# A hybrid decoder layer on one core: the conv tiles' sum on other queues, half-wide products in pairs, the square root's table at other places

## The chip, the cores and the metric

The kernel runs on one core of one Trainium2 chip. A core has a matrix engine (TensorE, "PE" in the profile; its weight loads are the row "PEld"), a vector engine (VectorE, "DVE"), an activation engine (ScalarE, "ACT"), GpSimd ("POOL") and SyncE ("SP"), which here only issues DMAs. Each engine takes its instructions strictly in the order in which the program gives them, and engines wait for each other through semaphores. DMAs are issued from SP, ACT or POOL and run on 16 DMA engines. The metric is the device time of one execution in microseconds (us).

## The reference

One layer with batch 1, 1024 tokens and width 1024, all in float32:

```
h = rmsnorm(x) * (1 + scale(c)) + shift(c)
cv, cg, cs, lx, ls = split(h @ W_in)            # five times 1024 columns
v = layernorm(causal_conv31(cv * sigmoid(cg)))  # depthwise, 31 taps
y_conv = (silu(v) @ pw2 + b) * silu(cs)
xs = causal_conv4(lx)
r, i = sigmoid(blockdiag(xs)), sigmoid(blockdiag(xs))
a = exp(-8 r softplus(-lam))
y_lru = scan(a, sqrt(1 - a^2) * i * xs) * silu(ls)
x = rmsnorm(x + (1 + gate(c)) * (concat(y_conv, y_lru) @ W_out))
```

## The kernel before

**Layout.** Channels lie on the 128 partitions and the 1024 tokens along them, so that a matrix of 1024 channels is eight tiles of 128 x 1024. Tiles come from pools: 47 `big` buffers, two buffers each for a slot's weights (`raw`, `whi`, `wlo`), three PSUM tiles `mm` of two banks and two PSUM tiles `acc` of one bank.

**Products.** To keep float32's precision each operand is split into a rounded part and a remainder (`uh`, `ul`; `whi`, `wlo`), and a product is three matmuls: hi x hi, hi x lo, lo x hi. A *slot* is one tile of 128 output columns: 8 k-tiles x 3 terms x 2 halves = 48 matmuls of 512 columns (L506). For a slot's weights SP loads `raw`, ACT casts it to `whi` (L355), and the remainder `wlo` is a subtraction on POOL (slots under `EARLY` = 20), on DVE (under `LATE` = 41), or, in the last slots, ACT writes -`whi` into `wlo` and POOL issues a DMA that adds the source from DRAM (`remainder`, L387).

**Stages.** First four tiles of W_in are multiplied while x arrives, with the norm's factor applied later. The factor is found on the way: squares, a matmul with ones (`token_stats`), a square root on ACT (`root`), a reciprocal on DVE, a matmul that spreads it (L934), a copy to `rbc`; a fifth accumulation (`late`) follows. Then come slots 4 to 39 in the sequence `ORDER` ("i24" is column tile 24 of W_in, "g0" the gates of head 0), slots 40 to 47 (the lru half of W_out, from `yh`, `yl`), and then pw2 and the conv half of W_out as pairs of tiles, with seven half-size products for eight (tiles `xpw`, `zpw`, `ypw`, `xout` and so on). Column tiles 0-7 are conv values, 8-15 their gates, 16-23 `cs`, 24-31 `lx`, 32-39 `ls`.

**Conv.** Each of eight conv tiles is taken apart into even and odd tokens. Five accumulate their taps on DVE (`cacc`, `caccs`). Tiles 1, 3 and 5 (`POOLED`, function `conv_pooled`) do it by DMA: ACT writes each tap's product into a buffer (`cq`, both halves; `co`, one half of a buffer), and POOL issues a DMA that adds it to `es` or `oo` (function `ADD`, L387). `conv_sum` then adds the eight tiles into `csum`, in the order 2, 3, 0, 1, 7, 4, 5, 6: POOL does all additions but the last, DVE that one. `layer_norm` splits `csum`, finds the mean with a matmul, subtracts it, sums the squares in `lnss`, and takes a square root (`rstd`) for the factor `lnbc`.

**The order.** All this is first written down as operations with a priority, a cost and their reads and writes. At build time the class `Plan` plays them through in modelled time: whenever an engine is free it takes, of the operations that are ready and find free buffers, the one with the lowest priority number, and that becomes the program's order on each engine. So a changed cost or dependency can move any operation of any engine. `LAND` is the flight that the plan takes for a remainder's DMA, `FLIGHT` that of the other adding DMAs, `SWITCH` that of a table load on ACT; `reserve` asks for free `big` buffers beyond the operation's own; conv operations have priorities from 1000 up, slots their number. Activation functions come in table sets, and where a function needs another set than the one loaded, an ACT_TABLE_LOAD stands before it.

Lines: L355 copies and casts on ACT, L363 activations and their table loads, L374 scalar_tensor_tensor on DVE, L382 tensor_tensor on DVE or POOL, L387 adding DMAs on POOL, L401 DMAs on SP, L506 slots, L675 pair products, L799 first products, L981 the product `psbias` that sums `fsum`, L1205 gate products, L1242 the layer norm's mean.

Of the kernel before, what the change touches and what calls it, by code (L numbers as in the profile page):

```python
# [77 lines left out]
SUMS = (2, 3, 0, 1, 7, 4, 5, 6)  # L78
QRES = 0
# [13 lines left out]
LATE, LAND = 41, 4.5  # L93
# [32 lines left out]
class Plan:  # L126
# [4 lines left out]
    SWITCH = 1.3  # L131
# [56 lines left out]
    def order(self):  # L188
# [48 lines left out]
        while left:  # L237
# [3 lines left out]
            for e in engines:  # L241
# [29 lines left out]
                if o.table and o.table != table:  # L271
                    cost, table = cost + self.SWITCH, o.table
# [38 lines left out]
def hymba_layer(ctx: ExitStack, tc: tile.TileContext, xT, vecs, mod_w, w_first, w_in,  # L311
# [182 lines left out]
    def weights(s, after=(), n=None, eng=None, where=None, late=()):  # L494
        n = number[s] if n is None else n
        eng = eng or ("POOL" if n < EARLY else "DVE" if n < LATE else "DMA")
        w_bufs(s, where)
        w_slice(s, 0, KT, n - 2.5, n - 1.4, after, eng, late)
# [206 lines left out]
    def rstd(prio, sqs, a, e, ps, o, after=(), warm=(), idle=None):  # L705
# [20 lines left out]
        for k, sq in enumerate(sqs):  # L726
            at = S.op("PE", 0.18 * nb, lambda sq=sq, k=k: stats(sq, k), prio, halves(sq, a, e), wk,
                      after=after if k == 0 else [])
            for _ in range(warm[k] if warm else 0):
                S.op("PE", 0.22, warm_mm, prio, [], [idle], after=[at], columns=4 * P)  # L730
# [22 lines left out]
    ACT(-101, lambda: junk, lambda: eps_t, AF.Sqrt, 1, r=[("cs", 0)], w=[("junk", 0)])  # L753
# [229 lines left out]
    S.op("PE", 0.18 * len(FIRST + NEXT), shift_mm, BIP, [fsum], [psx])  # L983
# [25 lines left out]
    def softplus8(pr, after):  # L1009
        lam = lambda: V[:, OFF["lam"]:OFF["lam"] + KT]  # L1010
        u, s, s2, q, r = (S.buf("sp_" + n, "sp_" + n) for n in ("u", "s", "s2", "q", "r"))
        ACT(pr, u, lam, AF.Abs, KT, w=[u])
        ACT(pr, u, u, AF.Exp, KT, scale=-1.0, r=[u], w=[u])
# [91 lines left out]
    def conv_pooled(i, pr, ci, vi, src, wts, every):  # L1105
# [3 lines left out]
        es, oo, adds = big_buf(f"es{i}", parts=2), big_buf(f"oo{i}"), []  # L1109

        def product(to, z, r, x, key, scale, bias=None):
            ACT(pr, part(to, z * H + (0 if z else r), z * H + H), x,
                AF.Copy if bias is None else AF.Identity, H - (0 if z else r), bias=bias,
                scale=scale, r=[key, ("V", 1), ("wsum", 0)], w=[(to, z if to.parts > 1 else 0)],
                after=adds[-AHEAD:][:len(adds) // AHEAD][:1])
        for r in range(16):
# [3 lines left out]
            product(q, 1, r, part(ci, PAD - r, PAD - r + H), (ci, 0), ws(r),  # L1120
# [5 lines left out]
            q = oo if r == 0 else big_buf(f"co{i}_{r}")  # L1126
            product(q, 0, r, lambda r=r: od()[:, :H - r], vi, w(2 * r + 1))
            if r:
                adds.append(ADD(pr, part(oo, r, H), part(q, r, H), H, r=[oo, q], w=[oo]))
# [3 lines left out]
        def last(eng, o, a, e, src, off, op):  # L1133
            TT(pr, eng, lambda: every(o)()[:, a:e], lambda: every(o)()[:, a:e],
               part(src, off, off + e - a), op, e - a, r=[ci, src], w=[ci])
# [5 lines left out]
    def conv_sum():  # L1141
        for i in SUMS[1:]:
            a, eng = (c[SUMS[0]] if i == SUMS[1] else csum), "DVE" if i == SUMS[-1] else "POOL"
            TT(1000 + 5 * i, eng, csum, a, c[i], ALU.add, r=[a, c[i]], w=[csum])


    sig, sls, lru, y, scs_d, gw = {}, {}, {}, {}, {}, {}
    yh, yl = [None] * KT, [None] * KT
# [9 lines left out]
    def split(pr, hi, lo, full, eng="DVE", reserve=0):  # L1158
        ACT(pr, hi, full, "copy", r=[full], w=[hi], reserve=reserve and reserve + 1)
        SUB(pr, eng, lo, full, hi, r=[full, hi], w=[lo], reserve=reserve)  # L1160

    def evac_in(m, ps, n, b=None, rb=()):
# [15 lines left out]
        elif kind == LS:  # L1178
            sls[i] = big_buf(f"sls{i}")
            ACT(pr, sls[i], ps, AF.Silu, bias=b, r=[ps, *rb], w=[sls[i]])  # L1180
# [14 lines left out]
    def gates(i, n):  # L1195
# [27 lines left out]
        split(B0 - 2 + 0.2 * i, yh[i], yl[i], t, reserve=SPARE)  # L1223
# [11 lines left out]
    def layer_norm():  # L1235
# [9 lines left out]
        for t in range(KT):  # L1245
            TT(pr, "DVE", c[t], c[t], mean, ALU.subtract, r=[c[t], mean], w=[c[t]])
            if t == 0:
                ACT(pr, ss, c[t], AF.Square, r=[c[t]], w=[ss])
# [40 lines left out]
    n, started, acc_d = 3, {}, {}  # L1289
    for s in slots[4:]:  # L1290
# [5 lines left out]
        if s not in NEXT:  # L1296
            weights(s)
# [9 lines left out]
        for k in range(KT):  # L1307
            o = mm_k(n, ps, s, xh, xl, k, FULL)
            if k == 0:
                started[n] = o  # L1310
        if s[0] == "in":
# [6 lines left out]
            else:  # L1318
                evac_in(m, ps, n)
# [205 lines left out]
```

## Time and profile before

| | |
|---|---|
| median of 3 runs | 733.21 us (733.05 to 734.43) |
| profiled execution, its own time | 734.38 us |
| its span, first to last instruction | 732.5 us |
| granted TensorE clock, mean | 0.996 |
| busy: PE, PEld, DVE, ACT, POOL | 722.9, 601.2, 611.2, 459.4, 159.6 us |
| 16 DMA engines: moved over the span | 121.03 MB, mean 165 GB/s |
| ACT_TABLE_LOAD | 45, 1283 ns each |

The profile is of one execution. Its page gives busy times by engine, the span in 40 slices, the DMA queues, the chain of work that ended last, the costliest groups of instructions (line, engine, operation, out<-in names without buffer numbers) and the DMA issues. Rows of the timeline have the start, the length, the engine, the line, the operation, the tiles, their shape, the count of merged instructions, and in brackets the idle time before it with what ended it. A matmul's length includes its way through the pipeline, so successive matmuls overlap. The profiled execution's 734.38 us is 1.17 us above the median of the three runs.

### The profile page before, as it was taken

How to read it: one execution, taken by the hardware profiler on the slowest of the kernel's cores; microseconds unless marked ns; L12 is line 12 of the kernel's file. 1: busy time of each engine (PE TensorE's matmuls, PEld its weight loads, DVE VectorE, ACT ScalarE, POOL GpSimd, SP SyncE). 2: the span in 40 equal slices, each digit the busy share in tenths (PEclk: the TensorE clock that was granted, in tenths of full speed). 3: DMA queues.
4: the chain of work that ended last, by engine and by line, in shares of the span. 5: the costliest groups of instructions: out<-in, count | busy, mean ns of one | idle time of the engine just before them, and what ended most of it. 6: DMA issues, size and time to landing. Idle time of an engine off the chain costs nothing.

```text
span 732.5 us, 8976 instructions
## 1 busy us (share of the span) xinstructions
PE 722.9 (99%) x3292; PEld 601.2 (82%) x3292; DVE 611.2 (83%) x832; ACT 459.4 (63%) x579; POOL 159.6 (22%) x147
## 2 busy tenths in 40 slices
PE   9999999999999999999999999999999999999996
PEld 8888888888888887888888888888888888878885
DVE  7999999989559996888598999839698566999647
ACT  7650677656669759956848789517594345755322
POOL 0024012344524222232215111320000001010003
PEclk9999999999999999999999999999999999999998
DMA  8961023358888999799753644686666846784006
GB/s 342 408 223 58 0 82 84 86 115 191 196 209 183 239 243 215 179 224 211 161 114 85 154 90 120 173 233 174 170 158 152 227 117 138 221 217 167 20 15 216
DMA packets 40508, 121.03 MB, mean 165 GB/s; under 512 B 4496, under 2 KB 13200, under 8 KB 40464
## 3 DMA queue, kind: packets, MB, share of 16 engines
q0 software_dynamic: 15552, 43.70, 33.0%
q1 hardware_dynamic: 23904, 75.84, 30.3%
q10 hardware_dynamic: 1008, 0.92, 0.4%
q8 instruction: 26, 0.43, 0.2%
q14 instruction: 18, 0.15, 0.1%
HBM read 72.55 MB, written 12.58 MB: 116 GB/s over the span
## 4 chain that ended last, share of the span: by engine, by line
PE 69%; DVE 13%; issue 11%; DMA 3%; ACT 3%; POOL 1%; DVEq 0%; POOLq 0%; ACTq 0%
PE ps L506 46%; PE xout L675 5%; PE xpw L675 5%; PE ypw L675 3%; DVE modw L374 2%; DVE caccs L374 2%; PE gate L1205 2%; PE y L650 2%; PE zpw L675 1%; DMA wloout<-in_w_out_dram 1%; DVE ul L374 1%; DVE cacc L374 1%; PE zout L675 1%; DMA oo<-co 1%; DMA wlo<-in_w_out_dram 1%
## 5 line engine op out<-in xcount | busy, mean ns | idle before, releaser
L506 PE MATMUL ps<-uh,whi 128*128 128x512 f32 x576 | 177.6, 390 | 0.3 <-ACT scs L363 0.3
L506 PE MATMUL ps<-ul,whi 128*128 128x512 f32 x576 | 177.4, 389 | 0.0
L506 PE MATMUL ps<-uh,wlo 128*128 128x512 f32 x576 | 177.3, 389 | 0.0
L506 PEld LDWEIGHTS ps<-uh,whi 128*128 128x128 f32 x576 | 107.9, 188 | 23.3 <-ACT scs L363 1.0
L506 PEld LDWEIGHTS ps<-ul,whi 128*128 128x128 f32 x576 | 108.1, 188 | 22.5
L506 PEld LDWEIGHTS ps<-uh,wlo 128*128 128x128 f32 x576 | 108.1, 188 | 22.5
L355 ACT CAST whi<-raw 128x1024 fp32r<-128x1024 f32 x44 | 45.9, 1047 | 69.9 <-PE ps L506 44.9
L387 POOL DMA_DIRECT2D es<-cq x45 | 41.1, 936 | 128.0 <-ACT cq L363 91.7
L382 POOL TENSOR_TENSOR wlo<-raw,whi 128x1024 fp32r<-128x1024 f32 x16 | 40.3, 2530 | 126.0 <-ACT whi L355 85.1
L363 ACT ACT_TABLE_LOAD x45 | 57.7, 1283 | 5.8 <-DMA oo<-co 4.3
L374 DVE SCALAR_TENSOR_TENSOR cacc<-v,V,cacc 128x511 f32<-128x511 f32 (+14 forms) x75 | 55.6, 742 | 0.5
L374 DVE SCALAR_TENSOR_TENSOR caccs<-v,V,caccs 128x511 f32<-128x511 f32 (+6 forms) x70 | 52.1, 744 | 2.3 <-ACT caccs L363 1.1
L374 DVE SCALAR_TENSOR_TENSOR caccs<-c,wsum,caccs 128x511 f32<-128x511 f32 (+6 forms) x70 | 52.0, 743 | 1.0
L387 POOL DMA_DIRECT2D oo<-co x42 | 37.9, 948 | 61.7 <-ACT co L363 25.3
L506 PE MATMUL ps<-yh,wlo 128*128 128x512 f32 x128 | 39.6, 391 | 0.2 <-DMA wlo<-in_w_out_dram 0.2
L506 PE MATMUL ps<-yh,whi 128*128 128x512 f32 x128 | 39.6, 391 | 0.0
L506 PE MATMUL ps<-yl,whi 128*128 128x512 f32 x128 | 39.5, 389 | 0.0
L382 DVE TENSOR_TENSOR wlo<-raw,whi 128x1024 fp32r<-128x1024 f32 x21 | 27.5, 1311 | 5.8 <-ACT whi L355 5.8
L363 ACT ACTIVATE cq<-v,V 128x511 f32<-128x511 f32 (+14 forms) x45 | 31.8, 706 | 0.1
L374 DVE SCALAR_TENSOR_TENSOR xs<-ps,V,xs 128x1023 f32<-128x1023 f32 (+2 forms) x24 | 30.6, 1273 | 0.0
L374 DVE SCALAR_TENSOR_TENSOR modw<-modw,sc 128x1024 f32<-128x1024 f32 x23 | 30.1, 1312 | 0.0
L363 ACT ACTIVATE cq<-c,wsum 128x512 f32<-128x512 f32 x42 | 29.6, 711 | 0.0
(334 smaller groups left out, 1458.1 us busy)
## 6 DMA issues: line engine op xcount, KB each, us to landing
raw<-in_w_in_dram SPq DMA_DIRECT2D x36, 512.0 KB, 4.5
modw<-in_mod_w_dram SPq DMA_DIRECT2D x24, 512.0 KB, 7.9
scsd<-scs SPq DMA_DIRECT2D x8, 512.0 KB, 4.3
raw<-in_w_out_dram SPq DMA_DIRECT2D x8, 512.0 KB, 4.1
accd<-acc SPq DMA_DIRECT2D x8, 512.0 KB, 4.5
rawpw<-in_pw_dram SPq DMA_DIRECT2D x8, 512.0 KB, 4.1
scsr<-scsd SPq DMA_DIRECT2D x8, 512.0 KB, 4.9
rawout<-in_w_out_dram SPq DMA_DIRECT2D x8, 512.0 KB, 3.3
```

The costliest lines, as they stand in the source:

```text
L355: act.copy(out(), in_())
L363: act.activation(out=out(), in_=in_(), func=func, **kw)
L374: dve.scalar_tensor_tensor(out=out(), in0=in0(), scalar=scalar, in1=in1(), op0=op0, op1=op1, accum_out=accum)
L382: lambda: e.tensor_tensor(out=out(), in0=a(), in1=b(), op=op), prio, r, w,
L387: return S.op("POOL", ISSUE, lambda: pool.dma_start(out(), a(), accum_op=ALU.add), prio, r, w, lag=RATE * n / T, after=after, flight=flight)
L506: pe.matmul(ps()[:, a - off:b - off], k3(lhs)()[:, k, :], rhs[k]()[:, a:b], start=(k == 0 and lhs is wh and rhs is xh and (a - off) % H == 0),
L650: pe.matmul(to(), half(*lhs)()[:, j * P:j * P + P], half(*rhs)()[:, c0:c1], start=a == "S1" and j == 0 and t == 0, stop=j == KT // 2 - 1 a ...
L675: pe.matmul(half(ps, 0)(), half(*lhs)()[:, j * P:j * P + P], half(*rhs)(), start=start and j == 0 and t == 0, stop=j == KT // 2 - 1 and t ...
L1205: pe.matmul(ps()[:, c0:c1], lhs()[:, j, :], rhs()[:, c0:c1], start=st == 0, stop=st == 2)
```

## The change

- `conv_sum`: ACT copies conv tile 2 into `csum`; tiles 3, 0 and 1 are added by DMAs issued on POOL; tiles 7, 4, 5 and 6 (`CSD` = 4) are added on DVE. No tensor_tensor of POOL is left in the sum.
- `conv_pooled`: two odd-token products share one `big` buffer, one in each half (taps 0 and 1 in `oo` itself); ACT products ask for two spare `big` buffers (`CQR`).
- Softplus' Abs and Exp, which had the priority 35, get the priorities -129 and -128, and a one-element Sqrt (it loads the table) comes behind them, at -127. In `layer_norm` such a one-element Sqrt follows the first Square.
- The split of the lru outputs of heads 0 and 1 (`YHEADS`) waits for the start of slot 36 (`YSLOT`).
- Where an `ls` slot from slot 4 on is followed by gates, the ACT cast of the weights two and three slots on waits for that slot's evacuation (`pending_evac`).
- The plan's own figures: `LAND` 4.5 to 6.0, `SWITCH` 1.3 to 1.283 less the time that ACT has been idle, a one-column statistics matmul 0.18 to 0.224 us. The program's order is planned anew with all of this.

No matmul is added or removed, and `ORDER` is as it was. `EARLYD` is empty, so the kinds of remainders stay with their slots.

```diff
...
 SUMS = (2, 3, 0, 1, 7, 4, 5, 6)
+CSD = 4
+EVN = 4
+CQR = 2
+YHEADS, YSLOT = 2, 36
 QRES = 0
...
 EARLY = 20
-LATE, LAND = 41, 4.5
+EARLYD = ()
+LATE, LAND = 41, 6.0
 ISSUE, FLIGHT, RATE = 1.0, 10.0, 3.0
...
     LATENCY = {"SP": 2.0, "PE": 0.2, "ACT": 0.15, "DVE": 0.15, "POOL": 0.15}
-    SWITCH = 1.3
+    SWITCH = 1.283
     TICK, BUSY, COLD = 3.4133, 3060, 3.8
...
                 if o.table and o.table != table:
-                    cost, table = cost + self.SWITCH, o.table
+                    cost, table = cost + max(0.0, self.SWITCH - max(0.0, t - until[e])), o.table
                 if e == "PE":
...
         n = number[s] if n is None else n
-        eng = eng or ("POOL" if n < EARLY else "DVE" if n < LATE else "DMA")
+        eng = eng or ("DMA" if n in EARLYD or n >= LATE else "POOL" if n < EARLY else "DVE")
         w_bufs(s, where)
...
         for k, sq in enumerate(sqs):
-            at = S.op("PE", 0.18 * nb, lambda sq=sq, k=k: stats(sq, k), prio, halves(sq, a, e), wk,
+            at = S.op("PE", 0.224 * nb, lambda sq=sq, k=k: stats(sq, k), prio, halves(sq, a, e), wk,
                       after=after if k == 0 else [])
...
     ACT(-130, lambda: cs, lambda: V[:, OFF["c"]:OFF["c"] + KT], AF.Silu, KT, w=[("cs", 0)])
-    ACT(-101, lambda: junk, lambda: eps_t, AF.Sqrt, 1, r=[("cs", 0)], w=[("junk", 0)])
+    sp_u = S.buf("sp_u", "sp_u")
+    ACT(-129, sp_u, lambda: V[:, OFF["lam"]:OFF["lam"] + KT], AF.Abs, KT, w=[sp_u])
+    ACT(-128, sp_u, sp_u, AF.Exp, KT, scale=-1.0, r=[sp_u, ("cs", 0)], w=[sp_u])
+    ACT(-127, lambda: junk, lambda: eps_t, AF.Sqrt, 1, r=[sp_u], w=[("junk", 0)])
...
                       start=True, stop=True)
-    S.op("PE", 0.18 * len(FIRST + NEXT), shift_mm, BIP, [fsum], [psx])
+    S.op("PE", 0.224 * len(FIRST + NEXT), shift_mm, BIP, [fsum], [psx])
     ACT(BIP, lambda: bias, lambda: psx()[:, :len(FIRST + NEXT)], "copy", len(FIRST + NEXT), r=[psx],
...
         lam = lambda: V[:, OFF["lam"]:OFF["lam"] + KT]
-        u, s, s2, q, r = (S.buf("sp_" + n, "sp_" + n) for n in ("u", "s", "s2", "q", "r"))
-        ACT(pr, u, lam, AF.Abs, KT, w=[u])
-        ACT(pr, u, u, AF.Exp, KT, scale=-1.0, r=[u], w=[u])
+        u = sp_u
+        s, s2, q, r = (S.buf("sp_" + n, "sp_" + n) for n in ("s", "s2", "q", "r"))
         TS(pr, s, u, 2.0, None, ALU.add, r=[u], w=[s], after=after)
...
         (ev, od), (w, ws) = src, wts
-        es, oo, adds = big_buf(f"es{i}", parts=2), big_buf(f"oo{i}"), []
+        es, oo, adds = big_buf(f"es{i}", parts=2), big_buf(f"oo{i}", parts=2), []
         def product(to, z, r, x, key, scale, bias=None):
-            ACT(pr, part(to, z * H + (0 if z else r), z * H + H), x,
-                AF.Copy if bias is None else AF.Identity, H - (0 if z else r), bias=bias,
-                scale=scale, r=[key, ("V", 1), ("wsum", 0)], w=[(to, z if to.parts > 1 else 0)],
+            ACT(pr, part(to, z * H + r, z * H + H), x,
+                AF.Copy if bias is None else AF.Identity, H - r, bias=bias,
+                scale=scale, r=[key, ("V", 1), ("wsum", 0)], w=[(to, z)], reserve=CQR,
                 after=adds[-AHEAD:][:len(adds) // AHEAD][:1])
                     None if r else vec("dw_b", i))
-            product(q, 1, r, part(ci, PAD - r, PAD - r + H), (ci, 0), ws(r),
+            product(q, 1, 0, part(ci, PAD - r, PAD - r + H), (ci, 0), ws(r),
                     None if r else bias2[:, i:i + 1])
                 continue
-            q = oo if r == 0 else big_buf(f"co{i}_{r}")
-            product(q, 0, r, lambda r=r: od()[:, :H - r], vi, w(2 * r + 1))
+            z = r % 2
+            q = oo if r < 2 else co if z else big_buf(f"co{i}_{r}", parts=2)
+            co = q
+            product(q, z, r, lambda r=r: od()[:, :H - r], vi, w(2 * r + 1))
             if r:
-                adds.append(ADD(pr, part(oo, r, H), part(q, r, H), H, r=[oo, q], w=[oo]))
+                adds.append(ADD(pr, part(oo, r, H), part(q, z * H + r, z * H + H), H,
+                                r=[(oo, 0), (q, z)], w=[(oo, 0)]))
         ACT(pr, every(1), half(es, 1), "copy", H, r=[es], w=[ci])
             TT(pr, eng, lambda: every(o)()[:, a:e], lambda: every(o)()[:, a:e],
-               part(src, off, off + e - a), op, e - a, r=[ci, src], w=[ci])
+               part(src, off, off + e - a), op, e - a, r=[ci, (src, off // H)], w=[ci])
         last(FOLD, 1, 0, H, es, 0, ALU.subtract)
     def conv_sum():
+        a = c[SUMS[0]]
+        ACT(1000 + 5 * SUMS[1], csum, a, "copy", r=[a, c[SUMS[1]]], w=[csum])
         for i in SUMS[1:]:
-            a, eng = (c[SUMS[0]] if i == SUMS[1] else csum), "DVE" if i == SUMS[-1] else "POOL"
-            TT(1000 + 5 * i, eng, csum, a, c[i], ALU.add, r=[a, c[i]], w=[csum])
+            if i in SUMS[-CSD:]:
+                TT(1000 + 5 * i, "DVE", csum, csum, c[i], ALU.add, r=[csum, c[i]], w=[csum])
+            else:
+                ADD(1000 + 5 * i, csum, c[i], r=[csum, c[i]], w=[csum])
     sig, sls, lru, y, scs_d, gw = {}, {}, {}, {}, {}, {}
+    waiting = []
     yh, yl = [None] * KT, [None] * KT
...
     def split(pr, hi, lo, full, eng="DVE", reserve=0):
-        ACT(pr, hi, full, "copy", r=[full], w=[hi], reserve=reserve and reserve + 1)
+        o = ACT(pr, hi, full, "copy", r=[full], w=[hi], reserve=reserve and reserve + 1)
         SUB(pr, eng, lo, full, hi, r=[full, hi], w=[lo], reserve=reserve)
+        return o
...
             sls[i] = big_buf(f"sls{i}")
-            ACT(pr, sls[i], ps, AF.Silu, bias=b, r=[ps, *rb], w=[sls[i]])
+            return ACT(pr, sls[i], ps, AF.Silu, bias=b, r=[ps, *rb], w=[sls[i]])
         else:
...
         yh[i], yl[i] = big_buf(f"yh{i}", F32R), big_buf(f"yl{i}", F32R)
-        split(B0 - 2 + 0.2 * i, yh[i], yl[i], t, reserve=SPARE)
+        o = split(B0 - 2 + 0.2 * i, yh[i], yl[i], t, reserve=SPARE)
+        if i < YHEADS:
+            waiting.append(o)
...
             if t == 0:
-                ACT(pr, ss, c[t], AF.Square, r=[c[t]], w=[ss])
+                o = ACT(pr, ss, c[t], AF.Square, r=[c[t]], w=[ss])
+                ACT(-1, lambda: junk, lambda: eps_t, AF.Sqrt, 1, w=[("junk", 0)], after=[o])
             else:
...
     softplus8(SPP, split_u[:1])
-    n, started, acc_d = 3, {}, {}
+    n, started, acc_d, pending_evac = 3, {}, {}, {}
     for s in slots[4:]:
...
         if s not in NEXT:
-            weights(s)
+            weights(s, late=[pending_evac[n]] if n in pending_evac else ())
         if GM <= n < GM + 8:
...
                 started[n] = o
+                if n == YSLOT:
+                    for x in waiting:
+                        S.hold(x, o)
         if s[0] == "in":
...
             else:
-                evac_in(m, ps, n)
+                o = evac_in(m, ps, n)
+                if m >= LS and n >= EVN and slots[slots.index(s) + 1][0] == "gate":
+                    pending_evac[n + 2] = pending_evac[n + 3] = o
             if m // KT * KT == CV:
```

## The prediction

> **What bounds the kernel now.** I read the page first, then PE's waits, then the busy time of stretches, then the timeline at each wait. The page:
>
> ```profile
> span 732.5 us, 8976 instructions
> ...
> PE 722.9 (99%) x3292; PEld 601.2 (82%) x3292; DVE 611.2 (83%) x832; ACT 459.4 (63%) x579; POOL 159.6 (22%) x147
> ```
>
> PE is busy for 722.9 of 732.5 us, so 9.6 us of the span are open to any change that leaves the matmuls alone. What they consist of is read from PE's waits, here all of them (who waited, for whom, us, times, longest):
>
> ```profile
> PE token_stats L756 <- DVE ones L432: 1.1, 1, 1.1
> PE finbc L724 <- DVE rs65.7_0_5731 L733: 0.9, 1, 0.9
> PE late L799 <- DVE first_u L382: 0.8, 1, 0.8
> PE xout L675 <- DMA wloout<-in_w_out_dram: 0.4, 1, 0.4
> PE ps L506 <- ACT scs L363: 0.3, 1, 0.3
> PE ps L506 <- DMA wlo<-in_w_out_dram: 0.2, 1, 0.2
> ```
>
> Together 3.7 us; the first row is the start and the second the last norm, neither touched by the diff in substance, and the remaining 5.9 us lie behind PE's last matmul. Four waits in the middle are left. Each costs more than its idle time:
>
> ```profile
> 51.35 0.50 PE L799 MATMUL late<-uh,fhi 128*128 128x512 f32 x1 [0.77 <-DVE first_u L382]
> 51.69 0.40 PE L799 MATMUL late<-uh,flo 128*128 128x512 f32 x1
> 51.92 0.40 PE L799 MATMUL late<-ul,fhi 128*128 128x512 f32 x1
> ```
>
> Matmuls start 0.23 us apart and last 0.40, so idle time is counted only once 0.17 of a missed start has gone by; and the first step after a wait is 0.34 instead of 0.23. A wait thus costs its idle time and 0.28 us. The four are worth 0.77 + 0.28 = 1.05 (`late`), 0.7 (`xout`), 0.6 (behind `scs`) and 0.5 (behind `wlo`): 2.85 us, 0.39% of the time. That is the most that a new order can gain in the middle; there is no such bound to what it can lose.
>
> DVE is the second bound, early on (a stretch's bounds and length, then busy time and count of PE, PEld, DVE, ACT and POOL, the granted clock, the DMA share and GB/s):
>
> ```profile
> 60.00:80.00 20.00, 20.00 (x90) 16.57 (x89) 19.61 (x38) 0.00 (x0) 3.53 (x3) 1.00 0.09 27
> ```
>
> PE has all 20 us and DVE 19.61, with the granted clock at 1.00: both are full at once, and DVE has 0.39 us to give.
>
> **The change part by part.**
>
> *The table of the first square root.* The rows around it, ACT at the start, then ACT, DVE and PE from 43 us:
>
> ```profile
> 3.05 1.28 ACT L363 ACT_TABLE_LOAD   x1
> 4.57 1.28 ACT L363 ACT_TABLE_LOAD   x1
> 5.86 0.21 ACT L363 ACTIVATE sp_u<-sp_u 128x8 f32<-128x8 f32 x1
> ...
> 43.20 1.28 ACT L363 ACT_TABLE_LOAD   x1
> ...
> 44.50 0.27 ACT L363 ACTIVATE st<-token_stats,eps_t 128x8 f32<-128x8 f32 x1
> ...
> 46.56 1.05 PE L934 MATMUL token_stats<-ident,st 128*128 128x128 f32 x8
> ```
>
> The one-element Sqrt loads the root's table at 3.05, and softplus' Exp (`sp_u`) throws it out at 4.57; so the root of the token statistics pays 1.28 us at 43.20. With Exp put first the start holds the same two loads, swapped, and costs nothing new: what follows on ACT begins at the same 6.07. The load at 43.20 goes. Root, spread (46.56) and the copies to `rbc` can then be up to 1.28 us earlier, and the `acc` buffer of `token_stats`, which `late` could take, is free before PE is done with the first products. `late` then has nothing to wait for: 1.05 us. The ends are 0 (PE's order puts the spread no earlier) and 1.05 (the whole stall); I take 1.05, since the load removed is longer than the stall. What is late next is the sum `fsum` for the product `psbias`, which DVE finishes shortly before:
>
> ```profile
> 84.74 0.34 DVE L374 SCALAR_TENSOR_TENSOR fsum<-raw,shift,fsum 128x128 f32<-128x128 f32 x1
> 85.51 1.62 PE L981 MATMUL psbias<-ones,fsum 128*128 128x1 f32 x14
> ```
>
> It is ready at 85.08, 0.43 before its use; a PE that is 1.05 ahead needs a place for it three matmuls later in its order, or DVE to gain as well. That is the first rival below.
>
> *The table of the layer norm's root.* `lnbc`'s square root:
>
> ```profile
> 511.40 1.28 ACT L363 ACT_TABLE_LOAD   x1
> 515.17 0.27 ACT L363 ACTIVATE sd-1_0_4068<-lnbc,eps_t 128x8 f32<-128x8 f32 x1 [2.48 <-PE lnbc L718]
> ```
>
> The load ended 2.48 us before PE's statistics did, so moving it gains nothing; one-element Sqrt and load, 1.5 us on ACT, lie among the squares, where ACT has idle time. Ends -0.2 to 0; I take 0.
>
> *The sum of conv tiles.* Its rows on POOL and DVE, with DVE's work beside it; the first groups five additions (ns min/median/max, first and last start):
>
> ```profile
> L382 POOL TENSOR_TENSOR csum<-csum,c x5: 2383/3245/3270, 387.2 to 478.2; 128x1024 f32<-128x1024 f32 x5
> ...
> 461.01 6.59 POOL L382 TENSOR_TENSOR csum<-csum,c 128x1024 f32<-128x1024 f32 x2 [3.58 <-DVE c L382]
> 462.71 2.63 DVE L382 TENSOR_TENSOR wlo<-raw,whi 128x1024 fp32r<-128x1024 f32 x1 [0.71 <-ACT whi L355]
> 476.77 1.29 DVE L382 TENSOR_TENSOR c<-c,oo 128x512 f32<-128x512 f32 x2
> 485.04 1.22 DVE L382 TENSOR_TENSOR csum<-csum,c 128x1024 f32<-128x1024 f32 x1
> ```
>
> Removed are six additions on POOL (these five and one before them); added are three on DVE (3 x 1.22 = 3.7 us), a copy on ACT (1.05, as the cast of this size at 520.77 below) and three DMAs on POOL. The tile that ends last is done at 478.06. From there two DVE additions give `csum` at 480.5 instead of 486.26, so the layer norm can start up to 5.8 us sooner. PE does not wait for it:
>
> ```profile
> 561.49 2.36 DVE L382 TENSOR_TENSOR l34pw<-rawpw,h34pw 128x1024 fp32r<-128x1024 f32 x2
> 565.09 0.39 PE L675 MATMUL xpw<-vha,whipw 128*128 128x512 f32 x1
> ```
>
> The DVE work that starts with the norm and ends with `l34pw` is done at 563.85; `l34pw` is first read two products (24 matmuls, 5.44 us) after 565.09, a reserve of 6.7 us. So the gain in the norm is worth 0. The adding DMAs take these times to land:
>
> ```profile
> DMA to landing us min/median/max: 3.3/6.3/11.6
> ```
>
> Three in a row, each waiting for the one before, take 19 to 35 us (3 x 6.3 to 3 x 11.6); POOL is in order, so an add of conv tile 5 behind them waits too. Before, the second addition, which needs tiles 2, 3 and 0, stood at 387.2, so three DMAs that begin about then end at 406 to 422, while the additions that DVE takes over were run from 461.01: hidden. Without that cover, tile 5 and with it the norm come 19 us later, less 5.8 and 6.7 of reserve: 6.5 us. I take 0 and keep it for the range.
>
> The pages weigh against a long flight: the Trainium skill, in "DMA: Bandwidth & Descriptors", section "Anatomy of one DMA — SWDGE (gpsimd) path", fits such a DMA with 2.0 us and its bytes at 436 GB/s, which as an estimate from that page is 3.2 us for 512 KB. By that figure the two waits for remainders below could not come from the flight and would stay, and the sum would be 732.2. The trace disagrees: the median is 6.3 us here, and 7.5 for `wlo`.
>
> *`LAND` and the remainders.* The wait for `wlo` at 533, from the cast on, and the flights (KB, median us from issue to landing):
>
> ```profile
> 520.77 1.05 ACT L355 CAST whi<-raw 128x1024 fp32r<-128x1024 f32 x1 [5.33 <-PE ps L506]
> 521.84 1.28 ACT L363 ACT_TABLE_LOAD   x1
> 523.13 1.25 ACT L363 ACTIVATE c<-c,V 128x1024 f32<-128x1024 f32 x1
> 524.28 1.04 ACT L363 ACTIVATE wlo<-whi 128x1024 fp32r<-128x1024 f32 x1
> 525.73 0.88 POOL L387 DMA_DIRECT2D wlo<-in_w_out_dram  x1 [15.25 <-ACT wlo L363]
> ...
> wlo<-in_w_out_dram POOLq DMA_DIRECT2D x7, 512.0 KB, 7.5
> ```
>
> Between cast and remainder the norm's first Silu got in, with its table: 1.28 + 1.15 us. With the norm up to 5.8 us earlier that Silu is past before 520.77, so the 0.5 us wait goes; ends 0 and 0.5, I take 0.5. The plan reckoned 1.0 + 4.5 = 5.5 us from issue to landing and now 7.0, against 7.5 measured; so it will put other products ahead of the one that waits for `wloout`, where there are any. Ends 0 and 0.7; I take the middle, 0.35.
>
> *The casts that wait for an evacuation.* The one late evacuation in the trace:
>
> ```profile
> 285.04 0.71 ACT L363 ACTIVATE co<-v,V 128x511 f32<-128x511 f32 x1
> 285.65 1.04 ACT L355 CAST whi<-raw 128x1024 fp32r<-128x1024 f32 x1
> 286.59 1.01 ACT L363 ACTIVATE scs<-ps 128x1024 f32<-128x1024 f32 x1
> 287.66 0.73 PE L506 MATMUL ps<-uh,whi 128*128 128x512 f32 x2 [0.33 <-ACT scs L363]
> ```
>
> A conv product and a cast stood ahead of an evacuation while two gate products held the other two `mm` tiles. The new wait is of this kind, but only for `ls` slots, and this is `cs` (slot 18, before g2). So the 0.6 us are not addressed: 0, ends -0.6 and +0.6. Behind the held cast stand its own subtraction and, a slot of 48 x 0.227 = 10.9 us later, PE; the cast moves by some 2.3 us (a table load and an evacuation).
>
> *Paired buffers, spare buffers, held splits.* These change no duration: the products and DMAs are the same in number and size. The two held splits are 2 casts and 2 subtractions that move to slot 36, four slots (43 us) before their first reader. They cost nothing while DVE's tail keeps its 6.7 us; without it, 2 x 1.22 us. The freed buffers (7 in each of three tiles) let ACT run products earlier; in price 0.
>
> **The sum.** 1.05 + 0.5 + 0.35 = 1.9 us. The profiled execution would take 734.38 - 1.9 = 732.5; the median shown, 1.17 below it, 731.3.
>
> **The rivals.**
>
> *DVE takes the gain back.* DVE has 0.39 us of idle time from 60 to 80 us, so `fsum` and what follows can move up by about 0.4 and no more; the rest of the 1.05 returns as a wait of `psbias` or slot 7. If the DMA waits stay as well, the gain is 0.4 and the time 732.8. For it: the 0.43 us above. Against it: PE can take other matmuls first, as it has slots 6 and 7 beside `psbias`.
>
> *Evacuations late at gates (slower).* From a slot's end the two gate products cover 12 x 0.227 = 2.7 us. A product (0.71), a cast (1.04), a table load (1.28) and an evacuation (1.01) in a row take 4.04: 1.3 idle and 0.28, 1.6 us a time. With more conv products ready on ACT, three of the eight gates would lose 4.8: 736.1. It decides from two on: 3.2 against 1.9 of gain. For it: 287.66 is such a wait, with 1.28 us of load less. Against it: four of the eight gates now have the cast moved away.
>
> *PE is not the bound.* If matmuls in the slots around 461 were paced by DVE, the time that POOL's additions took from it would come off in full: 2.63 at 462.71 against 1.22 without them, 1.4 us in the first half of the 6.59, 2.8 us in both: 728.5. The even 0.23 us between starts speaks against it. The Trainium skill, "Perfetto Trace Analysis", section "Identifying the Most-Contended Engine", holds that busy matmuls do not show the distance to the limit and weight loads do. By that rule the 82% of PEld would leave room; no row shows a start closer than 0.23.
>
> **How the numbers follow.** The likeliest case, 730.4 to 731.7 (its terms at their ends), has a chance of 0.45; DVE taking it back, up to no change, 0.29; gates or tile 5 late, 0.23; PE not the bound, 0.03. This kernel's measurement tells about 0.2%, 1.5 us, from no change. So faster has 0.48, the same 0.29, slower 0.23. The range, 730.2 to 736.0, goes from all four waits removed with 0.2 beside to three late gates.
>
> **What would show it.** Right: 44 table loads, none near 43 us; `late` without idle time; no POOL tensor_tensor on `csum`; `csum` done some 5 us sooner, PE's waits in the middle under 1 us. Wrong: a PE wait for ACT at gates, for `fsum` or `ul` near 85 to 100, or for a `v` tile at 565.

## The result, and the profile after

The changed kernel takes 731.79 us in the median (730.64 to 733.77, 22 runs), the kernel before 733.33 beside it (732.56 to 735.01, 22 runs). The ratio is 0.9976, with a 95% interval of 0.997 to 0.9983: 1.5 us between the medians, 1.2 to 2.2 us by the interval, so faster by little more than can be told from no change. The profiled execution has a time of 731.52 and this page:

```profile
span 729.7 us, 8957 instructions
...
PE 721.4 (99%) x3292; PEld 600.3 (82%) x3292; DVE 611.5 (84%) x835; ACT 460.0 (63%) x580; POOL 145.9 (20%) x144
...
L368 ACT ACT_TABLE_LOAD x44 | 56.5, 1283 | 2.5 <-issue 1.0
```

One table load is gone (44), three instructions left POOL (144), three came to DVE (835), and PE has its 3292 matmuls. PE's waits, all of them (who waited, for whom, us, times, longest):

```profile
PE token_stats L764 <- DVE ones L437: 1.1, 1, 1.1
PE finbc L729 <- DVE rs65.7_0_5712 L738: 0.9, 1, 0.9
PE ps L511 <- DMA wlo<-in_w_out_dram: 0.2, 1, 0.2
```

The waits of `late`, of `xout` and of `ps` behind `scs` are gone, and a wait for a `wlo` is still there. The timeline of the changed kernel around the place where `late` stood idle, ACT first, then PE:

```profile
42.72 0.25 ACT L368 ACTIVATE st<-token_stats,eps_t 128x8 f32<-128x8 f32 x1
42.87 0.69 ACT L368 ACTIVATE fsum<-raw,shift 128x128 f32<-128x128 f32 x2
...
44.46 1.05 PE L942 MATMUL token_stats<-ident,st 128*128 128x128 f32 x8
...
49.72 0.39 PE L807 MATMUL late<-uh,fhi 128*128 128x512 f32 x1
49.95 0.39 PE L807 MATMUL late<-uh,flo 128*128 128x512 f32 x1
```

No load stands ahead of the root, the spread follows 1.74 us after it begins (2.06 before, from 44.50 to 46.56), and `late` starts without a bracket behind it, which is how this view shows idle time. The sum of conv tiles, on DVE and then the cast that reads it:

```profile
475.94 2.48 DVE L387 TENSOR_TENSOR csum<-csum,c 128x1024 f32<-128x1024 f32 x2
...
478.46 1.05 ACT L360 CAST csh<-csum 128x1024 fp32r<-128x1024 f32 x1 [4.11 <-DVE csum L387]
```

It is done at 478.4, 7.8 us sooner than the 486.26 of before.

To compare kernels I cut PE's work at moments that all of them have: the start of the first product, of the first `ps` (so that `late` lies between the two), of the first `xpw`, of the first `xout`, and the end of the span. Each column is the difference of two such starts in the timeline, in us; the time beside it is the median of the runs, and the ratio is to the kernel before, run beside it. For the unchanged kernel's second profile there is one time.

| kernel | first starts | first to `ps` | `ps` to `xpw` | `xpw` to `xout` | `xout` to end | time | ratio (95%) |
|---|---|---|---|---|---|---|---|
| before | 8.56 | 48.39 | 508.14 | 73.44 | 93.96 | 733.33 | 1 |
| before, a second profile (e0) | 7.52 | 48.50 | 507.15 | 73.44 | 93.40 | 731.9 | |
| after | 7.84 | 47.32 | 507.59 | 73.44 | 93.55 | 731.79 | 0.9976 (0.997-0.9983) |
| before + table (e1) | 8.13 | 47.32 | 511.67 | 73.44 | 93.68 | 735.98 | 1.0035 (1.0023-1.0047) |
| before + sum (e5) | 7.70 | 48.45 | 507.44 | 73.44 | 93.38 | 733.24 | 0.9998 (0.9988-1.0008) |
| before + table, sum (e10) | 7.79 | 47.34 | 510.50 | 73.44 | 93.77 | 733.52 | 1.0002 (0.9993-1.0012) |
| before + table, sum, pairs (e11) | 7.72 | 47.33 | 507.80 | 75.63 | 93.83 | 734.0 | 1.0014 (1.0005-1.0023) |
| after, table as before (e2) | 7.78 | 48.66 | 507.49 | 73.44 | 93.34 | 732.98 | 0.9995 (0.9986-1.0003) |
| after, sum on POOL (e3) | 7.37 | 47.32 | 507.61 | 73.44 | 93.50 | 732.22 | 0.9985 (0.9976-0.9993) |
| after, `LAND` 4.5 (e4) | 8.39 | 47.33 | 507.51 | 73.44 | 93.88 | 731.76 | 0.998 (0.997-0.9991) |
| after, casts not held (e6) | 7.91 | 47.34 | 507.63 | 73.44 | 93.64 | 732.85 | 0.9993 (0.9983-1.0004) |
| after, no pairs (e12) | 8.05 | 47.34 | 507.42 | 73.44 | 93.87 | 731.44 | 0.9974 (0.9965-0.9984) |
| after, splits not held (e13) | 7.65 | 47.34 | 507.32 | 75.60 | 94.43 | 734.01 | 1.0011 (1.0001-1.0021) |
| after, `cs` slots too (e7) | 8.45 | 47.33 | 507.12 | 73.44 | 93.70 | 731.52 | 0.9971 (0.996-0.9981) |

The second column falls into two groups, 48.4 to 48.7 with the load in its old place and 47.3 without it. That 1.1 to 1.3 us is the whole of the change's gain that a profile shows: against e0, the changed kernel loses 0.3 at the start, 0.4 in the third column (its one wait for a `wlo` lies there) and 0.15 in the last.

### The profile page after: what moved, and what is told of

It reads as the page before. It is cut to its first block, busy times and chain, and to the rows that moved or that the text cites. A ratio compares the mean times of both kernels' runs of the same rounds, so it can differ in the third digit from the quotient of the medians.

```text
span 729.7 us, 8957 instructions
## 1 busy us (share of the span) xinstructions
PE 721.4 (99%) x3292; PEld 600.3 (82%) x3292; DVE 611.5 (84%) x835; ACT 460.0 (63%) x580; POOL 145.9 (20%) x144
## 4 chain that ended last, share of the span: by engine, by line
PE 95%; DMA 2%; ACT 1%; DVE 1%; POOL 0%; issue 0%; DVEq 0%; POOLq 0%
PE ps L511 62%; PE xpw L680 6%; PE xout L680 6%; PE first L807 5%; PE ypw L680 3%; PE gate L1221 3%; PE y L655 2%; PE zout L680 1%; PE zpw L680 1%; DMA wlo<-in_w_out_dram 1%; PE yout L680 1%; DMA es<-cq 1%; PE late L807 1%; DVE o L379 1%; PE token_stats L764 1%; ACT cq L368 0%
## 5 line engine op out<-in xcount | busy, mean ns | idle before, releaser
L387 POOL TENSOR_TENSOR wlo<-raw,whi 128x1024 fp32r<-128x1024 f32 x16 | 40.8, 2561 | 123.4 <-ACT whi L360 90.7
L392 POOL DMA_DIRECT2D oo<-co x39 | 36.3, 947 | 72.1 <-ACT co L368 30.3
L387 DVE TENSOR_TENSOR wlo<-raw,whi 128x1024 fp32r<-128x1024 f32 x21 | 25.6, 1218 | 5.7 <-ACT whi L360 5.6
```

What stands on the lines that cost most here:

```text
L387: lambda: e.tensor_tensor(out=out(), in0=a(), in1=b(), op=op), prio, r, w,
L392: return S.op("POOL", ISSUE, lambda: pool.dma_start(out(), a(), accum_op=ALU.add), prio, r, w, lag=RATE * n / T, after=after, flight=flight)
```

## The experiments

By the prediction the gain is the load's wait and two waits for DMAs, and the other parts are free. By the rivals the gain returns on DVE, at the gates, or through the order, which the planner makes anew with every edit. In the rows below, `scs` and `sls` are the tiles into which ACT evacuates a `cs` or an `ls` slot, `xsh` and `xsl` are the rounded part and the remainder of `xs` for the gates, and `vlb` are remainders of the normed conv tiles. In the code, `...` stands for lines that are not shown.

**The unchanged kernel once more (e0)**

> The kernel before, unchanged, profiled once more. In the first two profiles the first product on PE starts at 8.56 us (before) and 7.84 us (changed), though the instructions ahead of it are alike; in both, the short matmuls ahead of it double their rate, at 7.1 us in one and at 5.0 us in the other. If that moment is a matter of the execution and not of the kernel, the first product starts at another time here (7.2 to 8.9 us), and from there to the first `late` matmul it takes 42.8 us again, to 0.1. If it is the kernel's doing, it starts at 8.56 again, to 0.1.

One execution, 731.9 us, span 730.0. PE's waits in it:

```profile
PE token_stats L756 <- DVE ones L432: 1.1, 1, 1.1
PE late L799 <- DVE first_u L382: 0.9, 1, 0.9
PE finbc L724 <- DVE rs65.7_0_5731 L733: 0.9, 1, 0.9
```

The same program, and the waits for `wlo` and `wloout` are not there; the one behind `scs` has shrunk to 0.01 us, below what the view lists. The first product begins at 7.52 us instead of 8.56, and from there to the first `late` it takes 42.93 us against 42.80: the moment of the start belongs to the execution, as I expected. The place where `wlo` was waited for at 533 us, POOL's issue and then the matmul that had waited:

```profile
524.36 0.88 POOL L387 DMA_DIRECT2D wlo<-in_w_out_dram  x1 [15.25 <-ACT wlo L363]
...
531.45 0.62 PE L506 MATMUL ps<-yh,wlo 128*128 128x512 f32 x2
```

Issue and use stand 7.1 us apart. In the first profile they would have stood just as far apart (525.73, and 531.46 + 1.36 = 532.82), but there the DMA landed 0.4 later than that. `wloout` is alike: its longest flight was 9.9 us in the first profile and 8.3 here. So of the four waits in the middle only that of `late` is in both profiles, and the two DMA waits that the sum counted depend on the flights of one execution.

**The table alone (e1), and the whole change without it (e2)**

```diff
# e1, in the kernel before
-    ACT(-101, lambda: junk, lambda: eps_t, AF.Sqrt, 1, r=[("cs", 0)], w=[("junk", 0)])
+    sp_u = S.buf("sp_u", "sp_u")
+    ACT(-129, sp_u, lambda: V[:, OFF["lam"]:OFF["lam"] + KT], AF.Abs, KT, w=[sp_u])
+    ACT(-128, sp_u, sp_u, AF.Exp, KT, scale=-1.0, r=[sp_u, ("cs", 0)], w=[sp_u])
+    ACT(-127, lambda: junk, lambda: eps_t, AF.Sqrt, 1, r=[sp_u], w=[("junk", 0)])
...
# e2 puts the lines of the kernel before back into the changed kernel
```

> The kernel before with softplus' Abs and Exp and the Sqrt behind them put first, and nothing else. My theory: 44 table loads, none near 43 us, `late` without idle time, and from the first product to the first slot 1.05 us less (47.35 instead of 48.40), which is kept to the end: ratio 0.9986. The rival that DVE takes the gain back: 0.4 us less at most, with a wait of PE for DVE between 80 and 105 us: ratio 0.9995 or above.

> The changed kernel with softplus' Abs and Exp at their old priority and the one-element Sqrt at -101. My theory: the load near 43 us is back, `late` waits 0.8 us again, and the first product to the first slot takes 48.4 us instead of 47.3; the time is 1.05 us above the changed kernel's, ratio to before 0.999. If the other parts carry the gain: no more than 0.4 us above the changed kernel.

e2 is 1.2 us slower than the changed kernel and no different from before (0.9995), with the wait back as `PE late L804 <- DVE first_u L387`, 1.1 us: the load is worth 1.2 us, and all else together nothing that can be measured. e1 has the same gain in the second column and yet is slower than before by 0.35%. I had expected 0.9986 and 44 loads; there are 45, for the load near 43 us is gone and another has come in the new order. e1 pays 3.5 us in the third column; the waits of e1 there that are new or longer:

```profile
PE gate L1207 <- ACT xsh L355: 2.0, 1, 2.0
...
PE ps L506 <- ACT scs L363: 0.7, 1, 0.7
PE gate L1207 <- DVE xsl L382: 0.6, 1, 0.6
```

Its timeline ahead of that gate, for POOL, DVE and ACT:

```profile
372.30 3.26 POOL L382 TENSOR_TENSOR csum<-c,c 128x1024 f32<-128x1024 f32 x1 [11.15 <-DVE c L382]
...
376.11 2.71 POOL L382 TENSOR_TENSOR csum<-csum,c 128x1024 f32<-128x1024 f32 x1
...
379.07 3.01 POOL L382 TENSOR_TENSOR csum<-csum,c 128x1024 f32<-128x1024 f32 x1
...
373.86 2.24 DVE L382 TENSOR_TENSOR c<-v 128x512 f32<-128x512 f32 x1
...
377.33 0.73 DVE L374 SCALAR_TENSOR_TENSOR caccs<-v,V,caccs 128x504 f32<-128x504 f32 x1
...
379.29 3.89 DVE L382 TENSOR_TENSOR wlo<-raw,whi 128x1024 fp32r<-128x1024 f32 x1
...
388.13 1.04 ACT L355 CAST xsh<-xs 128x1024 fp32r<-128x1024 f32 x1 [8.16 <-DVE xs L374]
```

The planner put `csum`'s additions on POOL beside the chain that makes `xs` for the gate. DVE's remainder took 3.89 us instead of the 1.22 of an undisturbed one, and ended 1.1 us after POOL's addition did (379.07 + 3.01 = 382.08; 379.29 + 3.89 = 383.18); the other blocked one ended 0.5 after POOL's (375.56, 376.10). So the cast `xsh` was late and PE waited. The kernel before has blocked rows too, up to 3.43 us for one that takes 1.22, and no wait of PE from them; what e1 adds is the place, ahead of a gate. The Trainium skill, "SBUF — State Buffer", section "Who interferes with whom", says that a DVE instruction with two SBUF inputs contends with a GpSimd instruction that reads SBUF, and that the ports they share are an exclusive lock. The trace agrees for these `tensor_tensor` rows. Of `scalar_tensor_tensor`, also with two tensors, it shows both: the `caccs` row above kept its 0.73 us beside the POOL addition from 376.11 to 378.82, while in the kernel before one of `modw`, 61.1 us into the span, took 3.42 us beside a POOL subtraction instead of 1.22. What tells the two apart, no run shows.

**The sum alone (e5), the table with it (e10), and the change without it (e3)**

```diff
# e5, in the kernel before; e10 has e1's edit as well; e3 puts the old loop into the changed kernel
+CSD = 4
...
+        a = c[SUMS[0]]
+        ACT(1000 + 5 * SUMS[1], csum, a, "copy", r=[a, c[SUMS[1]]], w=[csum])
         for i in SUMS[1:]:
-            a, eng = (c[SUMS[0]] if i == SUMS[1] else csum), "DVE" if i == SUMS[-1] else "POOL"
-            TT(1000 + 5 * i, eng, csum, a, c[i], ALU.add, r=[a, c[i]], w=[csum])
+            if i in SUMS[-CSD:]:
+                TT(1000 + 5 * i, "DVE", csum, csum, c[i], ALU.add, r=[csum, c[i]], w=[csum])
+            else:
+                ADD(1000 + 5 * i, csum, c[i], r=[csum, c[i]], w=[csum])
```

> The kernel before with the sum of the conv tiles on DMA and DVE; nothing else. My theory: by itself it is worth nothing, because before no wait of PE comes from POOL's additions: `late` still waits 0.8 to 1.1 us, the first product to the first slot takes 48.4 us, and the time is the kernel's before within 0.5 us; the sum is ready some 5 us sooner in the trace. The rival that POOL's additions cost DVE and so PE time everywhere: 1 us less or more.

> The kernel before with softplus first and with the sum of the conv tiles on DMA and DVE; nothing else. With softplus first alone, PE waited 2.0 and 0.6 us at a gate near 389 us, where POOL's additions of the sum ran beside DVE and one DVE subtraction took 3.89 us instead of 1.22. My theory: POOL's additions held DVE up there, so without them that wait is gone, DVE's subtractions near 380 us take 1.2 to 1.4 us again, and the table's 1.05 us remain: ratio 0.9982 to 0.9990. The rival that the wait came from the new order as such: a wait of PE of over 1 us at a gate remains, ratio above 0.9995.

> The changed kernel with the sum of the conv tiles on POOL as before (six additions there, one on DVE). My theory: the sum is ready some 5 us later, but PE's waits stay as they are, since DVE's tail behind the norm has 6.7 us in hand; the time is the changed kernel's, within 0.5 us (what a newly planned order may move). If PE were paced by DVE: 2.8 us more, spread over the slots from 380 to 480 us. If the earlier norm had cured the wait for wlo at 533 us: 0.5 us more, at that place.

e5 is no faster than before, and `csum` is done at 474.1 there. In e3 it is done at 483.9, 5.5 us later than in the changed kernel, with no wait of PE in the middle and the same columns; the interval of its ratio overlaps that of the changed kernel. The earlier norm is worth nothing to PE, as predicted. e10 shows the sum's second effect: without POOL's additions the gate's waits of e1 are gone, and the remainders on DVE between 360 and 410 us take 1.21 to 1.22 us each. But it missed the gain that I expected, for another wait has come, at the gates near 287 us (ACT, then PE):

```profile
283.34 0.72 ACT L364 ACTIVATE co<-v,V 128x501 f32<-128x501 f32 x1 [2.12 <-DMA es<-cq]
283.96 1.03 ACT L356 CAST whi<-raw 128x1024 fp32r<-128x1024 f32 x1
285.89 1.02 ACT L364 ACTIVATE scs<-ps 128x1024 f32<-128x1024 f32 x1 [0.90 <-DMA es<-cq]
...
286.97 0.73 PE L507 MATMUL ps<-uh,whi 128*128 128x512 f32 x2 [1.62 <-ACT scs L364]
```

ACT stood twice for an adding DMA that still held a conv buffer, and the evacuation behind it came 1.62 us late for PE. This is the prediction's slower rival, in one place, and through adding DMAs, which that rival did not name.

**The pairs: added to e10 (e11), and taken from the change (e12)**

```diff
# e11, in e10's kernel (with the matching keys, and reserve=CQR, 2, on the products);
# e12 takes the same lines out of the changed kernel, the reserve too
...
-        es, oo, adds = big_buf(f"es{i}", parts=2), big_buf(f"oo{i}"), []
+        es, oo, adds = big_buf(f"es{i}", parts=2), big_buf(f"oo{i}", parts=2), []
...
+            z = r % 2
-            q = oo if r == 0 else big_buf(f"co{i}_{r}")
-            product(q, 0, r, lambda r=r: od()[:, :H - r], vi, w(2 * r + 1))
+            q = oo if r < 2 else co if z else big_buf(f"co{i}_{r}", parts=2)
+            co = q
+            product(q, z, r, lambda r=r: od()[:, :H - r], vi, w(2 * r + 1))
```

> The kernel before with softplus first, the sum on DMA and DVE, and the paired conv products with two spare buffers; nothing else. With the first two alone, ACT stood for adding DMAs (co 4.9, cq 1.1, scs 0.9 us) and PE waited 1.6 us for scs at 287 us. My theory: those ACT waits are for buffers that an add still reads, and pairing with two spare ones takes them away: under 1 us of such waits of ACT, no wait of PE for scs above 0.5 us, ratio 0.998 to 0.999. The rival that only the planned order matters and the buffers do not: a PE wait of over 1 us for ACT remains, ratio above 0.9995.

> The changed kernel without pairing and without the spare buffers. My theory: ACT waits for adding DMAs come back (3 us or more in all, against 0 in the changed kernel) and with them a PE wait for an evacuation at a gate, 0.6 to 2 us: ratio 0.9985 to 1.0005. The rival, as the prediction priced it: 0, within 0.5 us of the changed kernel.

I expected the pairs to be what frees ACT from the adding DMAs. In e11 the wait behind `scs` falls from 1.6 to 0.2 and the third column is 2.7 us shorter than e10's. But ACT still waits 4.9 us for adding DMAs, ahead of `yh` casts, a new wait of PE, for `vlb`, makes the fourth column 2.2 us longer, and the kernel is no faster than e10. In e12, without pairs, ACT does stand for adding DMAs again:

```profile
ACT cq L368 <- DMA es<-cq: 2.2, 1, 2.2
...
ACT L368 <- DMA oo<-co: 1.0, 1, 1.0
...
ACT co L368 <- DMA es<-cq: 0.5, 1, 0.5
```

The changed kernel has none of these. But the time of e12 is that of the changed kernel, and PE has no wait in the middle. The pairs take 3.7 us of waits from ACT and are worth nothing to PE; of what I expected of e12 the part on ACT held and the part on PE fell, and the prediction's 0 held.

**Holding the splits (e13) and the casts (e6)**

```diff
# e13, in the changed kernel
-YHEADS, YSLOT = 2, 36
+YHEADS, YSLOT = 0, 36
# e6, in the changed kernel
-            weights(s, late=[pending_evac[n]] if n in pending_evac else ())
+            weights(s)
```

> The changed kernel in which the splits of heads 0 and 1 wait for no slot. The prediction's price is 0: within 0.5 us of the changed kernel, no new wait of PE over 0.3 us. The rival: the splits take buffers and ACT time early, and PE waits for ACT between 150 and 300 us.

> The changed kernel without the wait of the casts for an `ls` slot's evacuation. My theory: 0, since no evacuation of an `ls` slot was waited for before; within 0.5 us of the changed kernel. The rival: at the gates behind slots 28, 32, 34 and 36 (340 to 450 us) PE waits for ACT, 0.6 us or more each.

e13 is 2.2 us slower than the changed kernel, and the interval of its ratio to before lies just above 1. PE's waits in it that the changed kernel has not, or has shorter:

```profile
PE zpw L680 <- DVE vlb L387: 0.9, 2, 0.5
...
PE ps L511 <- DMA wlo<-in_w_out_dram: 0.4, 1, 0.4
PE xout L680 <- DMA wloout<-in_w_out_dram: 0.4, 1, 0.4
```

The column from `xpw` to `xout` is 2.16 us longer. The timeline of e13's DVE and of its ACT, last conv products included:

```profile
473.18 0.71 ACT L368 ACTIVATE cq<-c,V 128x512 f32<-128x512 f32 x1
...
507.88 5.74 DVE L387 TENSOR_TENSOR c<-c,mean 128x1024 f32<-128x1024 f32 x5 [2.18 <-PE mean L1260]
...
568.17 1.24 DVE L387 TENSOR_TENSOR vlb<-c,vhb 128x1024 fp32r<-128x1024 f32 x1
571.71 1.24 DVE L387 TENSOR_TENSOR vlb<-c,vhb 128x1024 fp32r<-128x1024 f32 x1
```

and the same product and the same last tile of the changed kernel:

```profile
453.13 0.71 ACT L368 ACTIVATE cq<-c,V 128x512 f32<-128x512 f32 x1
...
547.32 1.22 DVE L387 TENSOR_TENSOR vlb<-c,vhb 128x1024 fp32r<-128x1024 f32 x1
```

The last conv product is 20.05 us later, `csum` ends at 498.9 instead of 478.4, the norm is as late, and the last two `vlb` end at 569.4 and 573.0 where `zpw`, which reads them, begins at 565.0. e11 has the same picture (`csum` 500.0, last `vlb` 573.5, 75.63). So the reserve on DVE's tail is real and can be used up: a norm 14 to 15 us later than before's (`c<-c,mean` at 507.88 and 507.66 against 493.09) costs PE 2.2 us, where one 2.2 us earlier (e3) or 7.3 us earlier (the changed kernel) gives it nothing. The late product goes with two things at once. In e13 the first `yh` is cast at 138.5, in the changed kernel at 248.3. But e10 casts it at 138.7 and has no late product; it has no pairs. The start of the last `cq` product, in us:

| | splits not held | splits held |
|---|---|---|
| without pairs and reserve | 456.96 (e10) | 448.35 (e12) |
| with both | 474.36 (e11), 473.18 (e13) | 453.13 (the changed kernel) |

So early splits delay it only where the products also come in pairs and ask for two spare buffers. That it is the reserve, which early splits leave unfilled since each holds two buffers, is argued only; no run has the pairs without the reserve.

e6 is 1.1 us slower than the changed kernel by the medians, but the intervals of the two touch (0.9983). Its ACT at the gate products near 388 us, and the matmul that waits:

```profile
385.79 1.05 ACT L360 CAST whi<-raw 128x1024 fp32r<-128x1024 f32 x1 [0.16 <-PE ps L511]
386.86 1.28 ACT L368 ACT_TABLE_LOAD   x1
388.16 1.02 ACT L368 ACTIVATE sls<-ps 128x1024 f32<-128x1024 f32 x1
...
389.24 0.72 PE L511 MATMUL ps<-uh,whi 128*128 128x512 f32 x2 [0.31 <-ACT sls L368]
```

and the same place in the changed kernel, where the load runs ahead and the cast follows the evacuation:

```profile
384.40 1.28 ACT L368 ACT_TABLE_LOAD   x1
386.47 1.03 ACT L368 ACTIVATE sls<-ps 128x1024 f32<-128x1024 f32 x1 [0.79 <-PE ps L511]
387.39 1.04 ACT L360 CAST whi<-raw 128x1024 fp32r<-128x1024 f32 x1
```

The held cast takes this wait away: 0.31 and 0.28, 0.6 us. The rest of the 1.1 is not in the profile: its third column is no longer than the changed kernel's, and the profiled execution, with 731.74 us, is near the fastest of e6's twelve (731.62 to 733.82).

**The planner's landing time (e4), and casts held in `cs` slots too (e7)**

```diff
# e4, in the changed kernel
-LATE, LAND = 41, 6.0
+LATE, LAND = 41, 4.5
# e7, in the changed kernel (evac_in returns the evacuation of a cs slot as well)
...
-                if m >= LS and n >= EVN and slots[slots.index(s) + 1][0] == "gate":
+                if m // KT * KT in (CS, LS) and n >= EVN and slots[slots.index(s) + 1][0] == "gate":
```

> The changed kernel with LAND at 4.5. My theory of the prediction: PE waits for wloout again near 652 us, 0.35 to 0.7 us. The rival, after the second profile of the kernel before, in which neither wlo nor wloout was waited for: those waits are a matter of the single execution, and nothing changes beyond 0.4 us, with PE's order near 652 us the same as in the changed kernel.

> The changed kernel in which the casts behind a `cs` slot that is followed by gates wait for its evacuation too, as they do behind an `ls` slot. What may be gained is the wait for scs at 228 us, 0.1 us idle and 0.28 with it, so 0.4 us at most: ratio 0.997 to 0.998. The rival: the newly planned order puts other waits in its place, 0.5 us or more.

e4 takes 731.76 us, as the changed kernel: the landing time has no effect that can be measured. e7 has the shortest third column of all, 507.12, and 731.52 us, which the intervals don't tell from 731.79. No version beat the changed kernel by an amount that can be measured.

## Why the prediction was right, and which of its steps were not

- **The total and its main term.** 731.3 was forecast and 731.79 measured, inside the range of 730.2 to 736.0, which also held no change and a loss. The load's term, 1.05, measured 1.2 between e2 and the changed kernel, and 1.1 to 1.3 in the second column. Its reason held too: `late` waited only because the root came late.
- **The term for `wlo` (0.5).** The step failed: the wait was an accident of the flight, as e0 shows, and a wait of this kind, 0.2 us, stands in the changed kernel for another `wlo`. What the step said of the Silu was half right: its table load has left the place between cast and remainder, but one Silu (1.24 us at 520.52) still lies there.
- **The term for `wloout` (0.35).** The step failed: the wait is absent in e0, with the old order, and again in e4, with the old `LAND`; and e13, with the new `LAND`, has it, 0.4 us.
- **What makes up for the two is luck.** The sum counted them against the profiled time of before, 734.38, which stood 1.05 above the median; that execution had both waits and began its first product at 8.56, the latest of all. So an excess of that execution was taken off twice, as a gain and as its distance to the median. The load's term alone makes 733.21 - 1.05 = 732.2; the 0.3 to 0.4 us by which the measurement lies below that, no run explains. It is as much as e2, without the load's gain, lies below the kernel before (732.98 and 733.33), which its interval does not tell from nothing.
- **The bounds of the likeliest case.** 730.4 to 731.7 was to hold the terms at their ends, but 731.7 is 731.3 with the term for `wloout` alone at 0. With that for `wlo` at its own end, 0, as well, it is 732.2. So the 731.79 lies outside the case as written, and inside it as its terms give it.
- **The zeros.** For the sum and the pairs they held. The norm's table no run takes out alone; in the changed kernel its root starts at 506.57 with no load ahead of it, and PE has no wait there. Nor does a run take back the plan's figures `SWITCH` and 0.224. For the held splits, "they cost nothing" held, but the zero left out what they are for: with the pairs in place and the splits not held, e13 loses 2.2. The prediction asked what each part adds to the old order, and the pairs make a new one in which early splits hurt. e10, with neither, has 73.44 us from `xpw` to `xout`, and e12, with the hold alone, is as fast as the changed kernel: there the hold makes up for what the pairs cost. No run takes both out of the changed kernel. For the held casts (0, ends -0.6 and +0.6), e6 loses 1.1 by the medians, of which 0.6 is seen in its profile.
- **DVE takes the gain back.** Fell: no wait for `psbias`, `fsum` or `ul` near 85 to 100 us in any run, and the 47.3 of the second column is not given back by the tail.
- **Evacuations late at gates.** Not in the changed kernel, but it is what e10 pays (1.62 us), and e6 in a small way. The condition named for it, two such places, is met nowhere in full; e10's one place, with a wait for `wlo` (0.5 us) and one behind `sls` (0.3 us), was enough to leave it at 1.0002.
- **PE is not the bound.** Fell: in the order of the changed kernel POOL's additions, there or not, change no column (e3: 507.61 us against 507.59), and in all twelve profiles without a wait from `xpw` to `xout` that stretch is 73.44 us.

## What to carry to other kernels

On an engine that is busy 99% of the time, take two profiles of the unchanged kernel before a wait of half a microsecond is priced: the one that stayed here (`late`) was worth what it showed, and the two DMA waits that came and went brought nothing that a run shows. The table load that was worth moving stood on the chain that the bound engine waited for, and its move cost nothing since two loads at the start could swap places. In an order that a planner makes anew, a part of a change cannot be priced alone: the part that brings the whole gain made the kernel 0.35% slower when added alone, and one part (the held splits) gains something only where another (the pairs) is there. Take single parts out of the finished version as well as adding them to the old one.

## What the runs showed of the hardware

PE's first, short matmuls run at one of two rates, and the moment of the change moves from run to run. In the timeline of PE at the start of the changed kernel, eight take 2.08 us (0.26 each) and, further on, sixteen of the same form 1.95 (0.12 each); the sixteen between them are shown of e3 and e7 too (in this order), which differ from it only further on:

```profile
1.06 2.08 PE L764 MATMUL token_stats<-ones 128*128 128x128 f32 x8 [1.06 <-DVE ones L437]
3.06 2.93 PE L768 MATMUL c_row<-ident,cs 128*128 128x128 f32 x16
5.83 1.95 PE L764 MATMUL token_stats<-ones 128*128 128x128 f32 x16
```

```profile
3.04 2.54 PE L768 MATMUL c_row<-ident,cs 128*128 128x128 f32 x16
```

```profile
2.95 3.75 PE L768 MATMUL c_row<-ident,cs 128*128 128x128 f32 x16
```

Over all fourteen profiles the `c_row` matmuls take 2.54 to 3.76 us, and the first product begins at 7.37 to 8.56, late where they are slow, in kernels that are alike up to there as in others. The granted clock does not show the change: in all fourteen it stands at 1.00 in every microsecond of the first ten. The Trainium skill, "TensorE: Matmul & The Clock Gate", section "Part 1: The HAM clock gate (the "warmup" mystery)", has the clock released by a window of some 3.4 us that runs freely and does not start with the kernel. The trace agrees in the effect, with up to 1.2 us between executions; the window itself no run here shows. So 0.7 of the 2.8 us between the two first profiles' spans (732.5 and 729.7) are not the change's.
